# A decoder layer on one core: the inverse's result asked for later in TensorE's planned order, and the query and key banks read with precedence

## The chip, the core and the metric

The kernel runs on one core of a Trainium2 chip. Five engines work on their own queues, each in order: TensorE (PE: matmuls, with its weight loads shown as PEld), VectorE (DVE), ScalarE (ACT), GpSimd (POOL) and SyncE (SP, which issues most transfers). They meet at semaphores. The metric is device microseconds (us) of one execution, lower is better. The median of 3 runs of the kernel before is 672.64 us (671.25 to 673.0).

## The reference, cut to what matters

One layer (512 tokens, width 1024) has a mixer of three groups of heads and a feed-forward part. Only the mixer matters here:

```
h    = rmsnorm(x) ; proj = h @ w_in           # columns: A (RWKV-7), B (MoBA q,k,v), C (gated MLP)
A:   state = state*w_t + sa (kk_t a_t)^T + v_t k_t^T ;  sa = -state kk_t ;  y_t = state r_t   # 6 heads of 64, over 512 steps
B:   attention, 6 heads of 64: softmax(q k^T / 8, causal over the selected blocks) @ v
C:   u * (W_s LN(v) + b), W_s causal 128 x 128, in 4 groups
x    = x + rmsnorm(concat(A, B, C) @ w_out)
x    = x + rmsnorm((silu(h2 @ w_gate) * (h2 @ w_up)) @ w_ffn_out)
```

With 512 tokens there are two blocks of 256, so that attention over the selected blocks is plain causal attention. The recurrence A is computed in 8 chunks of 64 tokens. In each chunk and head the substitutions (I - L)^-1 for a strictly lower triangular 64 x 64 matrix L are needed: 24 matrices of two heads, solved together before the chain over the chunks begins.

## The kernel before, in words

Every matmul of a projection is done three times to keep float32's precision in a faster format: a weight is split into a high part `wh` and a remainder `wl`, the activations into `bigh` and `bigl`, and wh.bigh + wh.bigl + wl.bigh are summed in a PSUM bank. One **dense step** below is such a group of three matmuls of 128x512 over one of eight blocks of the contraction. A projection of 128 columns (`dense_fm`) is eight dense steps into one of two banks called `acc`, taken in turn. Before it, `Feed` loads the 512 KB of weights into one of two buffers `wf`, ACT writes `wh` (two halves, L183), DVE writes `wl` (L185); `wh` and `wl` have two buffers each too.

**The order on TensorE** is fixed by the program. `Order` holds a modelled clock `t` that grows with each matmul's columns; side work (the recurrence, attention, the gated MLP) stands in generators that yield either a time to wait on that clock or the name of an event. Between two dense steps `pump` lets those whose time has come put their matmuls in. So a yield of 25000 means: the next matmuls of this generator come once matmuls of about 25 us have been put in front of them. Nothing in it knows what the other engines do.

**The inverse** (`inverse`). DVE transposes the diagonal 32 x 32 blocks into `tinv` (L650), runs 30 substitution steps there (L659, L662), and transposes the result back, into `tr` (L666) and `ca` (L667). Then the generator yields `T_INV`. After it TensorE does two rounds of 24 small matmul pairs for the off-diagonal block: `sb<-tr,p4` (two banks, copied out to `y` by ACT and DVE, L683), and `sb<-ca,y` (two banks, copied into `tt`, L709). Between the rounds ACT and POOL copy `ar` into `p4` (L692, L694). Event `inverse` lets the attention heads begin; `chain` follows at once: per chunk `rb<-sv,p4`, `rb<-rsb,tt`, `rb<-sv,bkt` with copies between them (L726, L744, L754).

**The queries and keys** (`dense_qk`). Six projections, q0, k0, q1, k1, q2, k2, run while DVE inverts and while the chain and the heads run. From q's bank ACT casts the rounded part into `qs` (L968) and DVE writes the remainder beside it (L970); from k's bank ACT casts `ks` (L976), POOL copies it to the other half (L978) and DVE writes the remainder `kl` (L980). A bank is free for the projection after the next once both have read it.

**The order on ACT, DVE, POOL and SP** is made by a scheduler that takes the ready instruction of highest priority by its own estimate of time, and leaves each queue in that order; `tc.high_priority(offset)` raises what is issued inside. The weights' splits have `PRI_W` = 20000, the recurrence `PRI_R` = 4000, and the reads of the q and k banks have none in the kernel before.

Of the kernel before, what the change touches and what calls it, by code (L numbers as in the profile page):

```python
# [8 lines left out]
F32 = mybir.dt.float32  # L9
# [3 lines left out]
OP = mybir.AluOpType  # L13
# [11 lines left out]
FF = 2816  # L25
FB = FF // 128
A_COLS = 1408
T_INV = 25000.0
T_TURN = 8500.0
T_SM, T_PT = 2400.0, 900.0  # L30
T_WD = 5000.0
# [9 lines left out]
PRI_W = 20000  # L41
# [55 lines left out]
def block_kernel(ctx: ExitStack, tc: tile.TileContext, x, pre_mix_g, w_in, rwkv_mu, rwkv_w0, rwkv_w2,  # L97
# [4 lines left out]
    act, dve, pool, sp = nc.scalar, nc.vector, nc.gpsimd, nc.sync  # L102
# [357 lines left out]
    def dense_fm(free=False):  # L460

        wh, wl = feed.next()
        wh = wh.rearrange("p (k c) -> p k c", k=KB)
        wl = wl.rearrange("p (k c) -> p k c", k=KB)
        p = acc()
        for k in range(KB):
            pe.matmul(p, wh[:, k], h1[:, k], start=(k == 0), stop=False)
            pe.matmul(p, wh[:, k], l1[:, k], start=False, stop=False)
            pe.matmul(p, wl[:, k], h1[:, k], start=False, stop=(k == KB - 1))
            if free:  # L470
                od.signal("free%d" % k)
            if k < KB - 1:
                od.pump()
        return p
# [28 lines left out]
    HR = [slice(0, 64), slice(64, 128)]  # L503
# [127 lines left out]
    def inverse():  # L631
# [36 lines left out]
        for h in range(2):  # L668
            for b in range(2):
                q = slice(64 * h + 32 * b, 64 * h + 32 * b + 32)  # L670
                (act.copy if b else dve.tensor_copy)(tt[q, :, 32 * b:32 * b + 32], tc_[q, :NP * NC, :])
        yield T_INV
        xo = tmp[:, :768].rearrange("p (u s) -> p u s", s=32)
# [289 lines left out]
    def dense_qk(b):  # L963

        qs, ks, kl = QK[b]
        p = dense_fm()
        for h in range(2):
            act.copy(qs[HR[h], h], p[HR[h]])  # L968
        for h in range(2):
            dve.tensor_tensor(qs[HR[1 - h], h], p[HR[h]], qs[HR[h], h].bitcast(F32), op=OP.subtract)  # L970
        od.pump()
        for h in range(2):
            pool.memset(kl[HR[1 - h], h].bitcast(F32), 0.0)
        p = dense_fm()
        for h in range(2):
            act.copy(ks[HR[h], h], p[HR[h]])  # L976
        for h in range(2):
            pool.tensor_scalar(ks[HR[1 - h], h], ks[HR[h], h].bitcast(F32), 1.0, 0.0, op0=OP.mult, op1=OP.add)  # L978
        for h in range(2):
            dve.tensor_tensor(kl[HR[h], h], p[HR[h]], ks[HR[h], h].bitcast(F32), op=OP.subtract)  # L980
        od.pump()
        od.signal("qk%d" % b, T_QK)

# [7 lines left out]
    AO = [ca.rearrange("p a b -> p (a b)")[:, :S], ca.rearrange("p a b -> p (a b)")[:, S:],  # L991
          ar[:, 0, 0:4].rearrange("p c a s -> p (c a s)")]
    dense_qk(0)
    dense_qk(1)
    dense_qk(2)
    p = dense_fm()
    shift(p, 10, sg)
# [20 lines left out]
    for b in range(2):  # L1018
        p = dense_fm(b == 1)
# [396 lines left out]
```

## Time and profile before

| what | value |
|---|---|
| median of 3 runs | 672.64 us (671.25 to 673.0) |
| the profiled execution's own time | 671.2 us |
| its span, first to last instruction | 669.5 us |
| PE busy | 644.1 us, 96% of the span |
| DVE busy | 450.3 us, 67% |
| ACT busy | 309.2 us, 46% |
| POOL busy | 58.7 us, 9% |
| mean granted TensorE clock | 0.988 |
| transferred | 61.25 MB, mean 91 GB/s |

What lies outside the span is 1.7 us of the execution's time. A busy share is a mean over stages with different limits: what a stage could give is read from the waits and the granted clock inside it. Matmuls overlap, so the distance from one start to the next tells more than one matmul's own duration.

### The profile page before, as it was taken

Reading aid. Unit: us, or ns where it says so; the run is one execution under the profiler, and the core shown is the slowest. Engines: PE = TensorE matmul, PEld = TensorE weight load, DVE = VectorE, ACT = ScalarE, POOL = GpSimd, SP = SyncE. Lnnn points to the kernel's source line nnn. Section 1 sums busy time; section 2 is a strip of 40 time slices with the busy share of each in tenths; the row PEclk is TensorE's granted clock in tenths of the full one; section 3 lists DMA queues with packets and bytes.
Section 4 is the critical chain, followed back from the end, with each engine's and each line's share of the span. In section 5 each row is a group of like instructions: output and inputs, shape, how many; then the busy total and the mean of one; then the engine's idle time right before and its main releaser. Section 6 shows DMA issues by size and latency. Waiting matters only on the chain.

```text
span 669.5 us, 11558 instructions
## 1 busy us (share of the span) xinstructions
PE 644.1 (96%) x4650; PEld 566.6 (85%) x4650; DVE 450.3 (67%) x779; ACT 309.2 (46%) x558; POOL 58.7 (9%) x107
## 2 busy tenths in 40 slices
PE   7998999699999999999999999999999999999996
PEld 6886779577777887878999999999999988888885
DVE  4699979946463769459897788788788575232214
ACT  6663443335554545437744554554554472132111
POOL 7120111121300100013000000000000000000001
PEclk9999999889999999999999999999999989999999
DMA  7422013311111117324534233333333024222303
GB/s 232 135 64 64 28 44 88 95 33 33 56 33 32 33 51 255 130 69 148 143 90 122 78 115 103 100 115 104 98 115 96 32 94 126 94 95 95 94 1 125
DMA packets 80901, 61.25 MB, mean 91 GB/s; under 512 B 2728, under 2 KB 70736, under 8 KB 80848
## 3 DMA queue, kind: packets, MB, share of 16 engines
q1 hardware_dynamic: 78800, 57.70, 28.1%
q10 hardware_dynamic: 2048, 2.82, 1.3%
q8 instruction: 36, 0.59, 0.4%
q14 instruction: 17, 0.14, 0.1%
HBM read 58.41 MB, written 2.10 MB: 90 GB/s over the span
## 4 chain that ended last, share of the span: by engine, by line
PE 76%; DVE 5%; issue 2%; ACT 1%; DMA 1%; POOL 0%; DVEq 0%; POOLq 0%; ACTq 0%
PE acc L112 29%; PE sb L112 29%; PE rb L112 6%; PE yb L112 6%; PE ob L112 5%; PE sb L117 1%; DVE wl L185 1%; DMA wf<-in_w_out_dram 1%; ACT wh L183 1%; DVE tinv L662 0%; DVE y L659 0%; DVE tinv L650 0%; DVE tr L666 0%; POOL rs L1137 0%; DVE x L1140 0%
## 5 line engine op out<-in xcount | busy, mean ns | idle before, releaser
L185 DVE TENSOR_TENSOR wl<-wf,wh 128x512 fp32r<-128x512 f32 (+2 forms) x82 | 73.4, 911 | 86.2 <-ACT wh L183 84.1
L183 ACT ACTIVATE wh<-wf 128x512 fp32r<-128x512 f32 (+2 forms) x82 | 63.6, 805 | 119.7 <-PE acc L112 34.1
L112 PE MATMUL sb<-h,wh 128*128 128x256 f32 x260 | 74.3, 286 | 2.2 <-DVE frow L1346 2.2
L112 PE MATMUL sb<-h,wl 128*128 128x256 f32 x260 | 74.1, 285 | 0.0
L112 PE MATMUL sb<-l,wh 128*128 128x256 f32 x260 | 74.0, 285 | 0.0
L112 PE MATMUL acc<-bigh,wh 128*128 128x512 f32 (+1 forms) x168 | 68.4, 410 | 0.8 <-ACT bigh L276 0.5
L112 PE MATMUL acc<-bigl,wh 128*128 128x512 f32 (+1 forms) x168 | 64.1, 386 | 0.3
L112 PE MATMUL acc<-bigh,wl 128*128 128x512 f32 (+1 forms) x168 | 59.6, 379 | 0.0
L1283 ACT ACTIVATE wh<-wf 128x1024 fp32r<-128x1024 f32 x38 | 39.9, 1058 | 38.9 <-DVE wf L1304 16.0
L1284 DVE TENSOR_TENSOR wl<-wf,wh 128x1024 fp32r<-128x1024 f32 x38 | 46.0, 1222 | 13.9 <-ACT wh L1283 13.9
L112 PEld LDWEIGHTS sb<-h,wh 128*128 128x128 f32 x260 | 50.2, 193 | 2.5 <-DVE frow L1346 2.5
L112 PEld LDWEIGHTS sb<-h,wl 128*128 128x128 f32 x260 | 50.3, 193 | 0.0
L112 PEld LDWEIGHTS sb<-l,wh 128*128 128x128 f32 x260 | 50.3, 193 | 0.0
L1137 POOL TENSOR_TENSOR rs<-rs,mhalf 128x1 f32<-128x1 f32 x8 | 7.3, 918 | 387.1 <-DVE rs L1132 383.8
L112 PEld LDWEIGHTS acc<-bigh,wh 128*128 128x128 f32 x168 | 32.1, 191 | 8.8 <-issue 2.0
L112 PEld LDWEIGHTS acc<-bigl,wh 128*128 128x128 f32 x168 | 32.2, 192 | 5.8 <-DVE bigl L277 0.9
L112 PEld LDWEIGHTS acc<-bigh,wl 128*128 128x128 f32 x168 | 30.2, 191 | 6.3
L1283 ACT ACTIVATE wh<-sums 128x1024 fp32r<-128x1024 f32 x19 | 20.1, 1060 | 29.7 <-PE acc L112 15.7
L1284 DVE TENSOR_TENSOR wl<-sums,wh 128x1024 fp32r<-128x1024 f32 x19 | 23.2, 1222 | 13.7 <-ACT wh L1283 13.7
L112 PE MATMUL acc<-l,wh 128*128 128x256 f32 x108 | 30.5, 283 | 0.8 <-DVE l L1168 0.8
L112 PE MATMUL acc<-h,wh 128*128 128x256 f32 x108 | 30.6, 283 | 0.0
L112 PE MATMUL acc<-h,wl 128*128 128x256 f32 x108 | 30.5, 282 | 0.0
(414 smaller groups left out, 1806.5 us busy)
## 6 DMA issues: line engine op xcount, KB each, us to landing
wf<-in_w_ffn_in_dram SPq DMA_DIRECT2D x76, 256.0 KB
wf<-in_w_ffn_out_dram SPq DMA_DIRECT2D x22, 512.0 KB
wf<-in_w_in_dram SPq DMA_DIRECT2D x21, 512.0 KB
wf<-in_w_out_dram SPq DMA_DIRECT2D x8, 512.0 KB
wf<-in_w_ffn_in_dram SPq DMA_DIRECT2D x6, 512.0 KB
xt<-in_x_dram SPq DMA_DIRECT2D x4, 512.0 KB
x<-in_x_dram SPq DMA_DIRECT2D x4, 512.0 KB
out_dram<-x SPq DMA_DIRECT2D x8, 256.0 KB
```

Source lines behind the costliest of these rows:

```text
L112: return nc.tensor.matmul(out_, lhsT, rhs, **kw)
L117: return nc.tensor.transpose(out_, in_, idn)
L183: act.activation(h[:, c], t[:, c], AF.Copy)
L185: eng.tensor_tensor(l[:, c], t[:, c], h[:, c].bitcast(F32), op=OP.subtract)
L1137: pool.tensor_tensor(r, r, mhalf[:, 0:1], op=OP.pow)
L1283: act.activation(h, src, AF.Copy)
L1284: dve.tensor_tensor(l, src, h.bitcast(F32), op=OP.subtract)
```

## The change

Two things are changed. `T_INV` goes from 25000 to 32500: 7.5 us more of modelled matmul time stand in front of the first matmul that reads the inverse. And the four kinds of reads of the q and k banks by ACT and DVE are issued with `PRI_W`; the remainder `kl` is issued ahead of POOL's copy of `ks`.

```diff
-T_INV = 25000.0
+T_INV = 32500.0
...
         p = dense_fm()
-        for h in range(2):
-            act.copy(qs[HR[h], h], p[HR[h]])
-        for h in range(2):
-            dve.tensor_tensor(qs[HR[1 - h], h], p[HR[h]], qs[HR[h], h].bitcast(F32), op=OP.subtract)
+        with tc.high_priority(offset=PRI_W):
+            for h in range(2):
+                act.copy(qs[HR[h], h], p[HR[h]])
+            for h in range(2):
+                dve.tensor_tensor(qs[HR[1 - h], h], p[HR[h]], qs[HR[h], h].bitcast(F32), op=OP.subtract)
...
         p = dense_fm()
-        for h in range(2):
-            act.copy(ks[HR[h], h], p[HR[h]])
+        with tc.high_priority(offset=PRI_W):
+            for h in range(2):
+                act.copy(ks[HR[h], h], p[HR[h]])
+            for h in range(2):
+                dve.tensor_tensor(kl[HR[h], h], p[HR[h]], ks[HR[h], h].bitcast(F32), op=OP.subtract)
         for h in range(2):
             pool.tensor_scalar(ks[HR[1 - h], h], ks[HR[h], h].bitcast(F32), 1.0, 0.0, op0=OP.mult, op1=OP.add)
-        for h in range(2):
-            dve.tensor_tensor(kl[HR[h], h], p[HR[h]], ks[HR[h], h].bitcast(F32), op=OP.subtract)
```

**TensorE at the first matmuls that read the inverse.** In the order before, the bank `acc_1370` is k0's; two of its eight dense steps stand ahead of the first group of `tr`:

```order
L112 MATMUL acc_1370<-bigh_80,wh_1364 128x512
L112 MATMUL acc_1370<-bigl_81,wh_1364 128x512
L112 MATMUL acc_1370<-bigh_80,wl_1365 128x512
L112 MATMUL sb_1377<-tr_1024,p4_401 32x32 x24
L112 MATMUL acc_1370<-bigh_80,wh_1364 128x512
L112 MATMUL acc_1370<-bigl_81,wh_1364 128x512
L112 MATMUL acc_1370<-bigh_80,wl_1365 128x512
L112 MATMUL sb_1407<-tr_1024,p4_401 32x32 x24
```

In the changed order the same place; `acc_1409` is q1's bank, and six of its eight dense steps stand ahead:

```order
L112 MATMUL acc_1409<-bigh_80,wh_1403 128x512
L112 MATMUL acc_1409<-bigl_81,wh_1403 128x512
L112 MATMUL acc_1409<-bigh_80,wl_1404 128x512
L112 MATMUL sb_1428<-tr_1024,p4_401 32x32 x24
L112 MATMUL acc_1409<-bigh_80,wh_1403 128x512
L112 MATMUL acc_1409<-bigl_81,wh_1403 128x512
L112 MATMUL acc_1409<-bigh_80,wl_1404 128x512
L112 MATMUL sb_1458<-tr_1024,p4_401 32x32 x24
```

The six remaining dense steps of k0 and six of q1, 36 matmuls, have moved from behind the first group of `tr` to ahead of it. No matmul is added or dropped.

**VectorE after the inverse.** Before, from the transposes on (`sb_1377` and `sb_1407` are the two banks of the first round, `sb_1454` and `sb_1484` those of the second; `wl_1676` is the remainder of k1's weights):

```order
L666 STREAM_TRANSPOSE tr_1024<-tinv_1025 128x32x32
L667 STREAM_TRANSPOSE ca_424<-tinv_1025 128x32x32
L671 COPY tt_1013<-ca_424 32x24x32 x2
L683 COPY y_1015<-sb_1377 32x384
L683 COPY y_1015<-sb_1407 32x384
L709 COPY tt_1013<-sb_1454 32x12x32
L709 COPY tt_1013<-sb_1484 32x12x32
L185 TENSOR_TENSOR wl_1676<-wf_1673,wh_1675 128x512 x2
```

Now (`wl_1511` is the remainder of k1's weights, `wl_1722` of q2's; the first round's banks are `sb_1428` and `sb_1458`, the second's `sb_1520` and `sb_1550`):

```order
L666 STREAM_TRANSPOSE tr_1024<-tinv_1025 128x32x32
L667 STREAM_TRANSPOSE ca_424<-tinv_1025 128x32x32
L185 TENSOR_TENSOR wl_1511<-wf_1508,wh_1510 128x512 x2
L980 TENSOR_TENSOR kl0_1316<-acc_1370,ks0_1315 64x512 x2
L671 COPY tt_1013<-ca_424 32x24x32 x2
L683 COPY y_1015<-sb_1428 32x384
L683 COPY y_1015<-sb_1458 32x384
L185 TENSOR_TENSOR wl_1722<-wf_1719,wh_1721 128x512 x2
L971 TENSOR_TENSOR qs1_1317<-acc_1409,qs1_1317 64x512 x2
L709 COPY tt_1013<-sb_1520 32x12x32
L709 COPY tt_1013<-sb_1550 32x12x32
```

Four instructions (the split of k1's weights, k0's remainder) now stand between the transposes and the copies that feed the second round, and four more (the split of q2's weights, q1's remainder) ahead of the copies into `tt`. Everything on DVE up to the transposes stands as it stood.

**ScalarE in the first two heads.** Now the split of k2's weights (`wh_1938`) and the cast of k1's bank stand between the copies of the two heads' first turned probabilities:

```order
L849 COPY pts0_1662<-sb_1660 128x128
L183 ACTIVATE wh_1938<-wf_1936 128x512 x2
L978 CAST ks1_1318<-acc_1516 64x512 x2
L849 COPY pts1_1686<-sb_1684 128x128
L838 ACTIVATE ee0_1671,mx0_1668<-sb_1664,mx0_1668 128x256
```

Before, a split and a cast (q2's weights, q1's bank) stand ahead of the second head's copy as well:

```order
L849 COPY pts0_1640<-sb_1638 128x128
L744 COPY sv_402<-rb_1653 64x3x64
L838 ACTIVATE ee0_1649,mx0_1646<-sb_1642,mx0_1646 128x256
L183 ACTIVATE wh_1925<-wf_1923 128x512 x2
L968 CAST qs1_1317<-acc_1552 64x512 x2
L849 COPY pts1_1687<-sb_1685 128x128
```

The two heads of a pair now run closer together: on TensorE one transposed block and one product of the second head stand right behind those of the first.

## Rows read from the trace of the kernel before

**Rows 1.** The page's first line.
```profile
span 669.5 us, 11558 instructions
```

**Rows 2.** Stretches: length, busy us (instructions) by engine, granted clock, DMA share, GB/s.
```profile
125.07:130.84 5.77, 0.01 (x1) 0.04 (x2) 5.52 (x15) 0.60 (x2) 0.00 (x0) 0.71 0.31 91
130.84:138.85 8.01, 8.01 (x154) 6.20 (x154) 4.20 (x5) 3.48 (x7) 4.09 (x9) 0.57 0.01 2
141.51:263.68 122.17, 121.72 (x1063) 95.76 (x1062) 77.93 (x200) 62.79 (x151) 16.77 (x21) 1.00 0.19 58
```

**Rows 3.** Waits of PE between 85 and 310 us: total, times, longest.
```profile
PE sb L112 <- DVE tr L666: 5.8, 1, 5.8
...
PE sb L112 <- DVE vg L908: 0.6, 1, 0.6
PE rb L112 <- DVE sv L744: 0.3, 1, 0.3
```

**Rows 4.** Timeline of PE around the wait: start, us, engine, operation [idle before].
```profile
123.97 0.39 PE L112 MATMUL acc<-bigh,wl 128*128 128x512 f32 x1
...
124.67 0.40 PE L112 MATMUL acc<-bigh,wl 128*128 128x512 f32 x1
130.84 1.49 PE L112 MATMUL sb<-tr,p 32*32 32x32 f32 x48 [5.77 <-DVE tr L666]
132.26 0.80 PE L112 MATMUL acc<-bigh,wh 128*128 128x512 f32 x1
...
133.84 1.49 PE L112 MATMUL sb<-tr,p 32*32 32x32 f32 x48
135.26 0.80 PE L112 MATMUL acc<-bigh,wh 128*128 128x512 f32 x1
...
137.97 0.95 PE L112 MATMUL sb<-ca,y 32*32 32x32 f32 x48
138.85 0.50 PE L112 MATMUL acc<-bigh,wh 128*128 128x512 f32 x1
...
139.74 0.95 PE L112 MATMUL sb<-ca,y 32*32 32x32 f32 x48
...
141.51 0.57 PE L112 MATMUL rb<-sv,p 128*64 128x64 f32 x12
```

**Rows 5.** Timeline of DVE, from the end of the inverse on.
```profile
125.94 1.39 DVE L970 TENSOR_TENSOR qs<-acc,qs 64x512 fp32r<-64x512 f32 x2
...
128.68 2.01 DVE L666 STREAM_TRANSPOSE tr<-tinv 128x1024 f32<-128x1024 f32 x1
130.55 1.91 DVE L667 STREAM_TRANSPOSE ca<-tinv 128x1024 f32<-128x1024 f32 x1
132.56 1.47 DVE L671 COPY tt<-ca 32x768 f32<-32x768 f32 x2
134.74 0.56 DVE L683 COPY y<-sb 32x384 f32<-32x384 f32 x1 [0.71 <-ACT y L683]
...
143.99 1.29 DVE L185 TENSOR_TENSOR wl<-wf,wh 128x512 fp32r<-128x512 f32 x2 [2.20 <-ACT wh L183]
145.58 1.39 DVE L980 TENSOR_TENSOR kl<-acc,ks 64x512 fp32r<-64x512 f32 x2 [0.30 <-ACT ks L976]
```

**Rows 6.** Timeline of ACT: a split, a cast, a copy of turned probabilities.
```profile
123.47 1.15 ACT L183 ACTIVATE wh<-wf 128x512 fp32r<-128x512 f32 x2 [3.88 <-PE acc L112]
124.53 1.16 ACT L968 CAST qs<-acc 64x512 fp32r<-64x512 f32 x2
...
156.22 0.27 ACT L849 COPY pts<-sb 128x128 f32<-128x128 f32 x1
```

**Rows 7.** Timeline of POOL: copies into p4, and two copies of ks.
```profile
134.56 2.53 POOL L694 TENSOR_SCALAR p<-ar 64x384 f32<-64x384 f32 x5 [0.94 <-PE sb L112]
...
175.00 1.12 POOL L978 TENSOR_SCALAR ks<-ks 64x512 fp32r<-64x512 f32 x1
...
176.80 0.61 POOL L978 TENSOR_SCALAR ks<-ks 64x512 fp32r<-64x512 f32 x1
```

## The prediction

> **What bounds the kernel now.** I read the stretches of the page first: TensorE is busy nearly everywhere, so only a place where it stands still, or runs at the lower clock, can give time. Next the list of who TensorE waited for. It has one large entry between 85 and 310 us: 5.8 us, once, for the transpose `tr` that ends the inverse; the next ones are 0.6 and 0.3 [rows 3]. Then the stretches around it: in the 5.77 us before the first `sb<-tr` TensorE does nothing while DVE is busy 5.52 of them; in the 8.01 us behind, TensorE is busy throughout at a granted clock of 0.57, mostly at 1.2 GHz, and from 141.51 us on for 122 us at 1.00, the 2.4 GHz level [rows 2]. Last the timelines. The reader is to see that the matmuls which follow the wait are late twice: they start 5.77 us late, and they run long. The chain of waits says the same from the other end: it leaves TensorE just here for DVE's substitutions and splits, and comes back to it at `sb<-tr`.
>
> What the low clock costs is read off starts. The first group of `tr` takes 130.84 to 132.26, 1.42 us, the second 133.84 to 135.26, also 1.42; the equally large groups of `ca` at full clock 0.88 (137.97 to 138.85). One dense step alone takes 1.58 (132.26 to 133.84) against 0.89 at full clock (138.85 to 139.74). The two dense steps from 135.26 to 137.97 take 2.71; at full clock they take 0.89 and 0.70, the pitch inside a run (123.97 to 124.67). So 0.54 + 0.54 + 0.69 + 1.12 = 2.9 us go to the clock, and 5.77 + 2.9 = 8.7 us to this place [rows 4].
>
> **The later request.** The order puts 12 dense steps ahead of the first `tr`. TensorE's run would have gone on at 124.67 + 0.23 = 124.90; 12 x 0.70 = 8.40 us later it is 133.30. `tr` ends at 128.68 + 2.01 = 130.69 [rows 4, 5], and nothing on DVE ahead of it has moved, so TensorE comes 2.6 us after it is ready and does not wait. The clock then has no reason to fall: TensorE has been busy up to there. With the full-clock prices above the new sequence (group, 1 step, group, 2 steps, group, 1 step, group, 1 step) takes 4 x 0.88 + 3 x 0.89 + 1.59 = 7.78 us, and the first `rb<-sv,p` starts at 133.30 + 7.78 = 141.08. Before it started at 141.51, with 12 dense steps fewer behind it. That is 0.43 + 8.40 = **8.8 us** ahead.
>
> What must hold for these 12 steps to run. q1 starts at about 124.90 + 6 x 0.70 = 129.1 in the bank that q0 used: DVE has read it by 125.94 + 1.39 = 127.3 [rows 5]. Its weights' split began at 123.47 on ACT [rows 6] and DVE's part stands where it stood. k1's first step comes at 133.30 + 0.88 + 0.89 + 0.88 + 0.70 = 136.65. It needs k1's split and k0's bank. ACT can begin the split at 129.1, when k0 ends, and takes 1.15 for it and 1.16 for k0's cast [rows 6], to 131.4. DVE is free of the transposes at 130.55 + 1.91 = 132.46, then 1.29 (split) to 133.75 and 1.39 (`kl`) to 135.14 [rows 5]: in time by 1.5 us. The loads move past nothing, SP's order being the same: after 130.84 hardly anything is transferred, 2 GB/s against 91 before [rows 2], so both weight buffers are full by then; the load for k1, one load of 0.5 MB / 91 GB/s = 5.8 us earlier, is in at about 125, ahead of the split at 129.1.
>
> **The reads with precedence.** They cost nothing by themselves: the same instructions, elsewhere in two queues. What is queued behind them counts. On DVE the copies of `tt` (1.47, to 136.6) and of the first bank into `y` (0.56, to 137.2) now stand behind the split and `kl`, and the first `sb<-ca,y` is due at 133.30 + 0.88 + 0.89 + 0.88 + 1.59 = 137.54 [rows 5]. So this is covered, by 0.3 us only; the second bank's copy (to 137.75) is due at 139.3. If ACT's cast comes late, TensorE waits as long as `kl` does; its 1.39 is the upper end, a slip of zero the lower one. I take zero, from the walk just made. On the other side, DVE's split and `kl` at 143.99 to 146.97 stood ahead of a copy for which TensorE waited 0.3 [rows 3, 5]; now they are earlier. **-0.3 us.**
>
> On ACT the split of k2's weights, the cast of k1's bank and then the second head's copy stand in a row: 1.15 + 1.16 + 0.27 = 2.6 us [rows 6] from the end of k1's last dense step, and TensorE wants that copy soon after, since both heads now run side by side. No row has this wait; before, a similar row of three on ACT made TensorE wait for nothing that the list shows [rows 3]. Bounds: 0 (all covered, as before) to 2.6 (none). TensorE has two chain groups, a score block and the first head's product to do meanwhile, some two thirds of it, so I take **+0.8**, and +0.3 for the like places later, where dense steps lie between.
>
> On POOL two copies of `ks` now come before the copies into `p4`: 1.43 us at 0.61 to 1.12 each are over by about 133.5, before those copies' own start (the first group of `tr` must be through). Before, the last five of them ended at 137.1, 4.4 us ahead of their first use [rows 7]; now they follow the `tr` groups by the same distance, about 2.5 us ahead. What POOL's copy costs beside DVE is seen at 175.00: 1.12 us against 0.61 at 176.80 for the same shape [rows 7]. The Trainium skill, "SBUF — State Buffer", section "Who interferes with whom", says that a VectorE instruction with two SBUF inputs and a GpSimd instruction that reads SBUF exclude each other, the later one being blocked for the whole of the other. The split of weights is such an instruction; by that rule POOL would wait out the new split at 132.46 to 133.75, which ends before POOL's copies of `p4` can begin, and the sum would stay; the 1.12 beside the 0.61 agrees with it.
>
> **Switching between kinds of matmuls.** A dense step in a run takes 0.70, one alone 0.89 [rows 4]: 0.19 for each interruption. Counted in the order from q0's start to the first output projection, the dense steps stand in 48 runs before and 44 now. Lower end zero (the first matmul behind an interruption might as well have been hidden), upper end 0.8; I take **-0.8**, since the 0.19 is read at just such interruptions.
>
> **The gated MLP's wait.** TensorE waited 0.6 for `vg` [rows 3], a long chain on DVE behind the last heads. The order has the last head 5 dense steps later and DVE's first item of that chain no later; it can vanish or double. I take 0, bounds -0.6 to +0.6.
>
> **Sum.** -8.8 - 0.3 - 0.8 + 0.8 + 0.3 = -8.8 us. The profiled execution took 671.2 us, 669.5 of span [rows 1] and 1.7 outside, which the change doesn't touch: 662.4. The runs' median is 672.64, 1.4 above that execution, so the median should be 663.8. With bounds: best -8.8 - 0.3 - 0.8 - 0.6 = -10.5, 662.1; worst -8.8 - 0.3 + 2.6 + 1.4 + 0.6 + 0.3 = -4.2, 668.4.
>
> **Rivals.** *The wait moves on (part of the gain goes).* The 0.3 us of cover at `sb<-ca,y` is gone and TensorE waits 1.4 there, and the full 2.6 at the second head: -8.8 + 4.0 = -4.8, 667.8. For it: DVE's and ACT's queues are in order, and four instructions were put before copies that TensorE waits for. Against: the walk above has each of them in time. 0.17.
>
> *The clock falls again.* TensorE gets many short waits in the heads and runs at 1.2 GHz for a while. One such episode cost 2.9 us [rows 4]: 666.7. Against it: 1.00 granted over 122 us of just this mixture [rows 2], with a wait of 0.3 in it [rows 3]. 0.07. The Trainium skill, "TensorE: Matmul & The Clock Gate", section "A second HAM failure mode: psum-queue depth-cycling", reports a kernel whose short idle spells between matmul groups let the clock swing. That rule would speak for this rival; the 122 us at 1.00 do not bear it out here.
>
> *The change doesn't do what it says.* DVE's inverse is itself put off by the reads with precedence, so that TensorE comes later and still waits 5.8: same time, 672.6. Against: up to `tr` DVE's order is unchanged. 0.05.
>
> *Slower.* The recurrence and the heads start 12 dense steps later in the order, so 8.4 us of matmuls that lay between their round trips to ACT and DVE are gone from the end of the mixer. If all of that was needed as cover, 8.4 us come back as waits behind the chain or the last heads, spread over places at each of which the clock may fall: 8.4 + 2.9 against 8.8 gives +2.5, 675. It decides from the point where later waits sum to more than 8.8 us. For it: nothing in the trace shows how much cover is to spare. Against: in 122 us TensorE idled 0.45 [rows 2], and the steps that moved stood around the first chunk, while each later chunk keeps dense steps or a head's matmuls between its groups. 0.05.
>
> **Chances and range.** Forecast 0.66, rivals 0.17, 0.07, 0.05, 0.05. About 0.3%, 2 us, is what a measurement of this kernel can tell from no change: faster than 670.6 are the forecast and the first two rivals, 0.89 with a little of the first one left out; same 0.06; slower 0.05. The range 661.5 to 668.5 holds the forecast with its bounds and the first two rivals' centres.
>
> **What would show it.** No wait of TensorE for `tr` and a granted clock of 1.00 between 125 and 141 us; 12 dense steps in one run there; the first `rb<-sv,p` near 141.1; from it on every stage 8 to 9 us earlier relative to the same matmul of before. A wait at `sb<-ca,y` for DVE's `y`, or one for the copy `pts` behind a cast, would show the first rival; slices with a clock under 1 after 141 us the second. The forecast is wrong if TensorE still stands over 2 us at `tr`, or if its waits between 141 us and the first output projection sum to over 4 us.

## The result, and the profile after

The changed kernel takes 665.56 us in the median of four executions (663.19 to 666.27), the kernel before beside it 672.82 (671.25 to 674.36): a ratio of 0.988, 95% interval 0.985 to 0.990, 7.3 us faster. The forecast was 663.8, a gain of 8.8. In a later comparison the two medians were 664.45 and 671.85, 0.9885 (0.9867 to 0.9904).

The page of the profiled execution (666.09 us): its span, and the granted clock in 40 slices.

```profile
span 664.4 us, 11553 instructions
...
PEclk8999999999999899999999999999999999999999
```

The stretches that answer to [rows 2]: length, busy us (instructions) of each engine, granted clock, DMA share, GB/s.

```profile
125.00:130.00 5.00, 5.00 (x23) 4.03 (x22) 4.25 (x15) 2.08 (x4) 0.00 (x0) 1.00 0.31 94
130.00:135.00 5.00, 5.00 (x31) 3.76 (x32) 4.97 (x5) 2.97 (x5) 1.24 (x2) 1.00 0.06 14
135.00:140.00 5.00, 5.00 (x154) 3.93 (x149) 4.85 (x9) 4.43 (x10) 4.25 (x9) 1.00 0.36 105
...
220.00:230.00 10.00, 10.00 (x60) 8.07 (x59) 4.37 (x13) 4.19 (x11) 2.27 (x1) 0.83 0.00 0
```

TensorE is busy throughout where it stood still, at a granted clock of 1.00, the 2.4 GHz level. The last row shows something new, a clock of 0.83 from 220 to 230 us. Whom TensorE waited for between 85 and 310 us, against [rows 3]:

```profile
PE acc L112 <- ACT gt L891: 1.7, 1, 1.7
...
PE ob L112 <- ACT pts L849: 0.6, 1, 0.6
...
PE sb L112 <- DVE y L796: 0.2, 1, 0.2
```

The waits for `tr`, `vg` and `sv` are gone; 1.7 for `gt` and 0.6 for `pts` have come. TensorE's timeline, against [rows 4]:

```profile
134.51 0.39 PE L112 MATMUL acc<-bigh,wl 128*128 128x512 f32 x1
134.83 0.95 PE L112 MATMUL sb<-tr,p 32*32 32x32 f32 x48
...
136.60 0.95 PE L112 MATMUL sb<-tr,p 32*32 32x32 f32 x48
...
139.07 0.95 PE L112 MATMUL sb<-ca,y 32*32 32x32 f32 x48
...
142.60 0.57 PE L112 MATMUL rb<-sv,p 128*64 128x64 f32 x12
...
152.48 0.43 PE L112 MATMUL ob<-pts,vt 128*64 128x128 f32 x2 [0.59 <-ACT pts L849]
...
258.38 0.50 PE L112 MATMUL acc<-wh,bigh 128*128 128x512 f32 x1 [1.69 <-ACT gt L891]
```

This execution was 1.4 us late already at q0's first dense step, from falls of the clock at 9 to 14 and 64 to 68 us, in code that did not change. Less those 1.4, `rb<-sv,p` starts at 141.2; 141.08 was forecast. DVE behind the inverse, against [rows 5]:

```profile
130.08 2.24 DVE L666 STREAM_TRANSPOSE tr<-tinv 128x1024 f32<-128x1024 f32 x1
132.22 2.04 DVE L667 STREAM_TRANSPOSE ca<-tinv 128x1024 f32<-128x1024 f32 x1
134.10 1.27 DVE L185 TENSOR_TENSOR wl<-wf,wh 128x512 fp32r<-128x512 f32 x2
135.41 1.39 DVE L980 TENSOR_TENSOR kl<-acc,ks 64x512 fp32r<-64x512 f32 x2
136.83 1.43 DVE L671 COPY tt<-ca 32x768 f32<-32x768 f32 x2
138.29 1.04 DVE L683 COPY y<-sb 32x384 f32<-32x384 f32 x2
```

`tr` is ready at 132.3, 2.5 us before it is asked for. The first half of the last copy, 0.5 us, ends at about 138.8, 0.3 ahead of `sb<-ca,y` at 139.07: the thin cover that the forecast named. Last, where 1.7 us were lost again, on ACT and on DVE:

```profile
257.73 0.60 ACT L891 ACTIVATE gt<-acc 128x512 f32<-128x512 f32 x1 [3.40 <-DVE u L895]
```
```profile
252.93 1.22 DVE L907 TENSOR_TENSOR vg<-vg,lng 128x1024 f32<-128x1024 f32 x1
254.07 1.29 DVE L802 TENSOR_TENSOR bigl<-ca,bigh 128x512 fp32r<-128x512 f32 x2
255.28 0.68 DVE L802 TENSOR_TENSOR bigl<-ar,bigh 128x512 fp32r<-128x512 f32 x1
255.88 1.22 DVE L185 TENSOR_TENSOR wl<-wf,wh 128x1024 fp32r<-128x1024 f32 x1
257.01 0.68 DVE L895 SCALAR_TENSOR_TENSOR u<-gt,u 128x512 f32<-128x512 f32 x1
```

The output projection's fourth bank is the one u1 was summed in. ACT frees it with L891, which writes the scratch tile `gt`; u0's last step L895 still reads `gt`, and on DVE it stands behind the five instructions shown above it. Two of them, L907 and the split L185 (1.22 us each), stood behind L895 in the kernel before (260.37 and 261.50 against 259.77). Even there ACT waited 1.78 us for this L895; TensorE did not feel it, because ACT was through 0.3 us before TensorE came (260.48 + 0.60 against 261.42):

```profile
260.48 0.60 ACT L891 ACTIVATE gt<-acc 128x512 f32<-128x512 f32 x1 [1.78 <-DVE u L895]
```
```profile
261.42 0.39 PE L112 MATMUL acc<-wh,bigh 128*128 128x512 f32 x1
```

### The profile page after: what moved, and what is told of

It reads as the page before. It is cut to its first block, busy times and chain, and to the rows that moved or that the text cites. A ratio compares the mean times of both kernels' runs of the same rounds, so it can differ in the third digit from the quotient of the medians.

```text
span 664.4 us, 11553 instructions
## 1 busy us (share of the span) xinstructions
PE 643.5 (97%) x4650; PEld 565.6 (85%) x4650; DVE 450.0 (68%) x779; ACT 308.9 (47%) x558; POOL 58.4 (9%) x107
## 4 chain that ended last, share of the span: by engine, by line
PE 77%; DVE 4%; ACT 1%; issue 1%; DMA 1%; POOL 0%; DVEq 0%; POOLq 0%; ACTq 0%
PE acc L112 30%; PE sb L112 29%; PE rb L112 6%; PE yb L112 5%; PE ob L112 4%; PE sb L117 1%; DVE wl L185 1%; DMA wf<-in_w_out_dram 1%; ACT wh L183 1%; DVE bigl L802 0%; DVE tinv L650 0%; POOL rs L1139 0%; DVE tinv L662 0%; DVE y L659 0%; DVE x L1142 0%
## 5 line engine op out<-in xcount | busy, mean ns | idle before, releaser
L185 DVE TENSOR_TENSOR wl<-wf,wh 128x512 fp32r<-128x512 f32 (+2 forms) x82 | 74.2, 921 | 83.3 <-ACT wh L183 83.0
```

Of the source, the lines that this page charges most:

```text
L185: eng.tensor_tensor(l[:, c], t[:, c], h[:, c].bitcast(F32), op=OP.subtract)
```

## The experiments

Theory: the later request gives nearly all, 5.8 us of wait and 3 us of clock behind it; the precedence gives next to nothing; a part comes back in the new waits. Rivals: the reads with precedence are what let the 12 steps run; or the clock's falls are chance and explain the rest.

**The two parts apart.**

```
late:  -T_INV = 25000.0    +T_INV = 32500.0     (nothing else)
prio:  with tc.high_priority(offset=PRI_W): round the four reads, kl ahead of POOL's ks   (T_INV 25000)
```

> Only the later request (T_INV 32500); the q and k banks are read in the order of the kernel before. TensorE's order is that of the changed kernel. Theory A (the request carries the whole gain, the precedence next to nothing): about 665.5 us, within 1.5 us of the changed kernel, no wait at the matmuls that read tr. Theory B (the 12 steps that now run ahead of tr need the banks of q and k to be read early): the wait comes back as a wait for an acc bank behind qs or kl between 125 and 141 us, 2 us or more, and the time is 668 us or more.

> Only the precedence of the q and k bank reads; the request stays at 25000. Theory A: the wait for tr stands as before (5 to 6 us, clock 0.5 to 0.7 behind it) and the time is within 1 us of the kernel before, about 672.5 us. Theory B: the waits shrink by 2 us or more and the time falls to 670 us or less.

The request alone: 664.85 us (663.88 to 666.73, six executions), 0.986 of the kernel before (0.982 to 0.990). The precedence alone: 673.86 against 674.55, 1.000 (0.997 to 1.003). The profile of the second shows the old wait, that of the first none, and the same loss at `gt`:

```profile
PE sb L112 <- DVE tr L666: 5.8, 1, 5.8
```
```profile
PE acc L112 <- ACT gt L891: 1.7, 1, 1.7
PE yb L112 <- DVE v L235: 1.1, 2, 0.7
PE ob L112 <- ACT pts L849: 1.1, 1, 1.1
```

The request carries it all. The precedence makes 0.5 us less of a wait for `pts` (1.1 against 0.6), too little for the times to show.

**The wait and the clock apart.** TensorE gets something to do where it waited, but nothing useful:

```
 px = sb()
+for _ in range(0 if hf else 25):
+    nc.tensor.matmul(px, h1[:, 0, 0:128], l1[:, 0], start=True, stop=True)
```

> The kernel before, request at 25000, with 25 matmuls of 512 columns into the bank that the tr matmuls are about to overwrite (0.23 us each, 5.8 us in sum; their results are used by nobody) put ahead of those matmuls. Nothing useful moves; TensorE is only busy where it used to wait. Theory A (the wait costs twice: its own 5.8 us, and then a low clock for 10 us or more of an execution): the wait falls under 0.5 us, the granted clock stays 1.00 from 125 to 145, the executions' mean clock rises from about 0.982 to 0.99, and the time falls by 3 to 5 us against the kernel before, though not one instruction less is done. Rival (the clock falls for a reason that lies in the work itself, or the waiting hides it): within 1 us of the kernel before, or slower.

> The changed kernel once more, beside the two others on one chip. All theories: 665 to 666 us, mean clock 0.99.

> The changed kernel with the second u block's scratch in wdad, once more beside the changed kernel on one chip. Theory A: the 1.7 us wait ahead of w_out counts in full, 1.5 us under the changed kernel in the mean of the executions. Rival: it is made up elsewhere, within 0.5 us.

The filled kernel takes 669.27 us against 671.85 beside it (0.9956, 0.9941 to 0.9971), less than the kernel before although it does more. Its rows at the place, timeline and then stretches:

```profile
125.71 5.87 PE L677 MATMUL sb<-bigl,bigh 128*128 128x512 f32 x25
131.83 0.95 PE L112 MATMUL sb<-tr,p 32*32 32x32 f32 x48 [0.26 <-DVE tr L666]
```
```profile
130.00:135.00 5.00, 4.74 (x108) 3.61 (x108) 4.65 (x4) 1.95 (x4) 2.56 (x5) 1.00 0.02 3
135.00:140.00 5.00, 4.87 (x109) 3.37 (x108) 1.98 (x4) 2.48 (x6) 1.93 (x5) 1.00 0.01 3
```

The clock stays at 1.00. The gain can also be read inside single executions, in the stretch from q0's first matmul to the first of the output projection (`w_out`). The first row is the kernel before, the second the filled kernel, the third the changed kernel in its second profile:

```profile
117.87:257.20 139.33, 133.11 (x1273) 104.38 (x1273) 88.04 (x237) 68.16 (x164) 20.86 (x30) 0.96 0.16 49
118.69:255.64 136.95, 136.10 (x1298) 107.04 (x1298) 88.02 (x237) 68.25 (x164) 21.31 (x30) 1.00 0.17 49
118.55:250.03 131.48, 130.61 (x1273) 101.79 (x1273) 87.23 (x239) 67.17 (x163) 20.78 (x30) 1.00 0.17 51
```

Without its 25 idle matmuls the filled kernel's TensorE is busy 136.10 - 5.87 = 130.23 us there, 2.9 less than before with the same 1273 matmuls: that is the clock. Of it 2.4 us are won in time (139.33 less 136.95), as the filling runs a little longer than the wait did.

On this one chip the means over executions differ by these steps (mean granted clock of the executions beside each):

| kernel | executions | mean us | clock | step |
|---|---|---|---|---|
| before | 13 | 672.04 | 0.985 | |
| before, wait filled | 8 | 668.85 | 0.994 | -3.2: the clock |
| changed | 5 | 664.01 | 0.994 | -4.8: useful steps in place of filling |
| changed, own scratch for u1 (below) | 5 | 663.11 | 0.995 | -0.9: the wait for `gt` |

Differences of four means in a row always add up to the whole, so the sum proves nothing. The last step is no larger than the spread of its executions, and the first two contain falls of the clock at other places too.

**The scratch tile.**

```
-gelu2(p, u2[:, b, :], gt)
+gelu2(p, u2[:, b, :], sg if b else gt)      (sg is the tile wdad, last read long before)
```

> The changed kernel, with the second u block's scratch moved from the shared tile gt into wdad, which nobody needs by then, so that its first ScalarE read (L891) need not wait for VectorE's last step of the first u block (L895). Theory A (that shared tile is the reason for TensorE's 1.7 us at the first acc<-wh,bigh of w_out): L891 starts when the bank is filled, about 3.4 us earlier, the 1.7 us wait is gone and the time is 1.5 to 2 us under the changed kernel's. Rival: the next reader is late instead (u1 and its to_mix are wanted a few us later), and the time stays within 0.5 us of the changed kernel's.

The wait is gone: the fourth bank's first matmul comes 4.2 us after the first bank's, where it was 6.1 (258.38 less 252.31), and without idle time. The timeline of this kernel's second profile:

```profile
250.75 0.40 PE L112 MATMUL acc<-wh,bigh 128*128 128x512 f32 x1
...
254.96 0.39 PE L112 MATMUL acc<-wh,bigh 128*128 128x512 f32 x1
```

In time it is 663.14 against 664.45 us beside it (ratios to the kernel before 0.9868, 0.9845 to 0.9891, and 0.9885, 0.9867 to 0.9904), and in the first comparison 664.68 against 664.85 of the request alone. It has the lowest median of all kernels beside it, both times, but the intervals overlap: by the times about 1 of the 1.7 us is likely and not proven, between the theory and its rival. Inside the profiles the wait counts in full: its first profile has the same three falls of the clock as the changed kernel's, at 9, 64 and 221 us, and one more of 1.7 us at 532, and both spans are 664.4 us: the missing wait makes up for the fall.

**Other times of the request.**

```
t280: T_INV = 28000.0 (5 dense steps ahead of tr)   t305: 30500.0 (9)   t450: 45000.0 (31)
```

> The changed kernel with the request at 28000: five dense steps of 0.69 us stand before the matmuls that read tr, against none before the change and twelve after it. Theory A (TensorE only has to have 5.8 us of other work there): the wait for tr is 5.8 - 5 x 0.69 = 2.3 us; one fall of the clock behind it, of the size seen after other waits of about 2 us (1.7 us lost), so 3 to 4 us over the changed kernel on the same chip. Rival (the clock, not the wait, is what costs: any wait there brings the full fall of some 10 us at 0.50 to 0.71): 2.3 us of wait and 3.5 us or more of low clock, 6 us or more over the changed kernel.

> The request at 30500: nine dense steps before the tr matmuls, 6.2 us of work against the 5.8 us of wait, so tr comes some 0.4 us before it is asked for. Theory A: no wait for tr over 0.3 us, clock 1.00 from 125 to 140, time within 0.7 us of the changed kernel. Rival (the chain wants to start as early as it can, since its end sets w_out): 1 us or more under the changed kernel, with the waits for gt and pts gone. Second rival (a cover this thin opens again in some executions): 1 to 3 us over it.

> The request at 45000: 31 dense steps before the tr matmuls, so the recurrence starts about 13 us later than in the changed kernel. Theory A (its end has slack, TensorE is full of dense steps either way): within 1 us of the changed kernel, no new wait over 1 us before 300 us. Rival (the later chain leaves too few dense steps at its end, and w_out waits for it): waits for y, sv, pts or the mixes of 3 us or more between 200 and 270 us, and 3 us or more over the changed kernel.

Beside a median of 672.39 of the kernel before: 669.15 (0.9966, 0.9943 to 0.9988), 666.76 (0.9915, 0.9886 to 0.9945) and 670.75 (0.9962, 0.9938 to 0.9986); the changed kernel was not in this comparison. With five steps the wait is 2.2 us, as worked out, but in the profiled execution (671.7 us of span) TensorE then runs at half the clock until 148, and is busy all the time from 135 on. From q0's first matmul to the output projection's it is busy 137.30 us, against 130.61 for the changed kernel at full clock: 6.7 us more.

```profile
PE sb L112 <- DVE tr L666: 2.2, 1, 2.2
```
```profile
130.00:135.00 5.00, 4.13 (x93) 3.35 (x95) 4.51 (x5) 3.02 (x6) 2.21 (x5) 0.57 0.01 3
135.00:140.00 5.00, 5.00 (x69) 3.83 (x66) 3.50 (x5) 3.09 (x7) 3.87 (x7) 0.50 0.35 103
140.00:145.00 5.00, 5.00 (x68) 3.32 (x67) 1.11 (x2) 0.63 (x2) 0.00 (x0) 0.50 0.02 5
145.00:150.00 5.00, 5.00 (x41) 4.07 (x40) 1.21 (x5) 1.09 (x4) 0.00 (x0) 0.72 0.00 0
```

Other executions of it took 665.4 to 672.0 of span at a mean clock of 0.992 to 0.981: how much clock follows a wait differs from one execution to the next. By the ratios (0.9966 against 0.9885 for the changed kernel in its own comparison) it stands 0.8% or 5.4 us over the changed kernel, between the two theories: neither has it whole. That the loss is so large in some executions and small in others leaves open what decides it.

With nine steps `tr` is not waited for, and I expected no wait at all. But TensorE then comes to `sb<-ca,y` 3 x 0.7 = 2.1 us earlier, while DVE's queue in front of the copies `y` is as long as in the changed kernel. Its timelines, TensorE's and DVE's, and the stretch behind:

```profile
136.45 0.24 PE L112 MATMUL sb<-ca,y 32*32 32x32 f32 x2
138.43 0.94 PE L112 MATMUL sb<-ca,y 32*32 32x32 f32 x46 [1.74 <-DVE y L683]
```
```profile
136.21 1.57 DVE L671 COPY tt<-ca 32x768 f32<-32x768 f32 x2
137.81 1.04 DVE L683 COPY y<-sb 32x384 f32<-32x384 f32 x2
```
```profile
140.00:145.00 5.00, 5.00 (x78) 3.77 (x77) 2.31 (x4) 2.66 (x5) 0.00 (x0) 0.54 0.00 0
```

1.74 us is about the forecast's cover of 0.3 less 2.1. By the ratios the time is 0.3%, 2 us, over the changed kernel's, the size of the second rival with another cause; the intervals overlap. With 31 steps the first pair of heads runs out of company: between 173 and 190 us TensorE has no dense step at all, it waits 3.2 us for a softmax, and the clock falls behind it (0.71 and 0.61 from 180 to 190).

```profile
182.24 1.11 PE L117 MATMUL sb<-ident,ee 128*128 128x128 f32 x4 [3.19 <-DVE ee L840]
```

So the request has a best stretch. Below it DVE's own queue is late, above it cover is missing later on. That is the mechanism of the forecast's slower rival, but at the first pair of heads, at 182 us, and not at the end of the mixer, where the rival and the expectation put it. At 45000 most of the gain is gone.

**The clock at 220 us.** It follows `sb<-hselm,sq`, 12 matmuls of two columns in one run of 1.5 us. They were cut into three runs (the loop is shortened here):

```
 for t in range(2): pe.matmul(pn[...], sq[...], hselm, start=True, stop=True)
+if p < NP - 1:
+    yield 1.0
```

> The changed kernel, with the 12 two-column matmuls of each rwkv_out (sb<-hselm,sq, 1.5 us in one run) cut into three runs of four with other matmuls between them. Theory A (the run of two-column matmuls is what makes the clock fall to 0.50 to 0.68 for some 3 us after it): no slice of granted clock under 1 between 210 and 235 us, and the time is up to 1.6 us under the changed kernel's, if that one's clock falls in most of its executions. Rival (the fall has nothing to do with that run, or it comes only in some executions): the time is within 0.5 us of the changed kernel's.

The time is 665.26 us, within 0.5 of the request alone (664.85); the changed kernel was not in this comparison. Its clock between 220 and 230 is 1.00, but so is that of the changed kernel's second profile, with the run of 12 whole (second row below):

```profile
220.00:230.00 10.00, 10.00 (x70) 8.00 (x69) 6.29 (x18) 4.51 (x12) 2.31 (x1) 1.00 0.17 52
220.00:230.00 10.00, 9.78 (x68) 7.68 (x67) 5.92 (x16) 4.34 (x10) 1.98 (x1) 1.00 0.16 52
```

Of the five profiles with the request at 32500 and the run whole, four show the fall and one does not, so one profile of the cut kernel does not tell whether the cut prevents it. Where the fall comes it costs 1.6 us: the stretch from q0's first matmul to the output projection's is 133.03 us in the changed kernel's first profile and 131.48 in its second. Undecided.

**Once more the kernel before.**

> The kernel before, once more, for a profile of one of its executions: its executions show granted clocks of 0.975 to 0.991 in the mean, while those with the later request show 0.988 to 0.998. Theory A: an execution at 0.980 or less shows the low clock behind the wait for tr lasting longer than the 10 us of the first profile, or more falls behind other waits, each worth 1.7 us. Rival: the falls lie at places that have nothing to do with waits.

This execution took 672.26 us at a clock of 0.983, not one of the lowest. Besides the fall behind `tr` it shows three short ones, at 9 to 14, 64 to 68 and 538 to 543 us, of which the first profile had only the last. Each takes 1.7 us of clock (its length times what is missing from a clock of 1), which is not always 1.7 us of time: q0's first matmul comes at 118.29 instead of 117.87 here, behind the first two of them. Where executions at 0.975 lose the rest was not caught.

## Why the prediction was right

- **The wait, 5.8 us.** Right: no wait for `tr`, twelve steps in one run, and `rb<-sv,p` 23.32 us behind q0's first matmul (142.60 less 119.28), where 141.08 less 117.87 = 23.21 was forecast.
- **The clock behind it, 2.9 us.** Right: the filled kernel's TensorE is busy 2.9 us less for the same matmuls, and its mean is 3.2 us lower. But it is no fixed price: the forecast read one execution, and in another a wait of 2.2 us was followed by a loss of 6.7.
- **The reads with precedence.** Right that they cost and give nothing that can be measured. The named risk, 0.3 us of cover at `sb<-ca,y`, held here and failed by the amount worked out when the steps were three fewer. The second head's `pts` cost 0.6, forecast 0.8.
- **Switching, -0.8.** Wrong in size and sign. Both at a clock of 1.00, the changed kernel's 1273 matmuls keep TensorE busy for 130.61 us and the same matmuls of the filled kernel for 130.23: some 0.4 us more, where 0.8 less was forecast for four interruptions fewer. The 0.19 read at single interruptions is thus not a price that fewer runs of dense steps give back; where the 0.4 goes is not shown.
- **The gated MLP, 0 (bounds -0.6 to +0.6).** The other step that missed. Its wait for `vg` went (-0.6), and one of 1.7 came beside it, at a place the walk did not visit: a scratch tile shared by two blocks, read by an instruction that slid back in DVE's queue. That is +1.1, outside its bounds.
- **The sum of these.** From q0's first matmul to the output projection's the changed kernel needs 131.48 us at full clock, 7.85 less than the 139.33 before; the sum said 8.8 by there. The difference is the switching (1.2 off), less 0.4 by which the new waits were smaller than forecast (idle 0.87 instead of 0.45, where the terms say 0.8 more).
- **The clock falls again** (0.07). In part, and not by that rival's way: the profiled execution has one such fall behind the new place, at 221 to 225, which costs 1.6 us, and it follows no wait. The Trainium skill, "TensorE: Matmul & The Clock Gate", section "What's actually happening", says that what the gate looks at runs free of the kernel's start; the same instructions at 220 with a clock of 0.83 in one execution and 1.00 in another agree with it.
- **The rival that the wait moves on** is priced wrongly: the -8.8 to which it adds 4.0 already holds 0.8 of its 2.6, so its time should have been 667.0 instead of 667.8.
- **The median** came out 1.8 us above 663.8 in the first comparison. That it came so near is in part luck. The two profiled executions differ by 5.1 us only (671.2 and 666.09): besides the terms above, the second has the falls at 9 and 64 (1.4 us) and at 221, and lacks one at 538. The medians differ by 7.3, as other executions of the kernel before lost more to the clock (0.985 in the mean against 0.994 on one chip), at places that were not caught.

## What to carry over

When a wait at one engine is filled by moving its work later, walk on to the end of the stage, through every tile that two steps share, not only to the next wait: here 1.7 us were lost 115 us further on, at a scratch tile. Look for such places in the trace of the kernel before, among the waits of the other engines that TensorE does not feel yet: this one stood there, with 0.3 us to spare. Price a wait of TensorE at its length plus a clock of 0.50 behind it, whose length varies from execution to execution, and test the two apart by filling the wait with idle matmuls. A request may come too early by the queue of the engine that answers it as well as by its first result: count what stands between the two.

## What was not expected of the hardware

Once fallen, the clock stayed at 0.50 with TensorE busy 5.00 of 5 us, for some 17 us in one execution (the rows of the request at 28000); behind the filled wait it did not fall at all. Short falls of some 4 us stood at the same few places (9, 64, 220, 538 us) in some profiles and not in others of the same instructions: that at 64 us follows a wait of 1.76 us, that at 538 one of 2.25, and that at 220 no wait, only the run of two-column matmuls.
